# ScalarE empties the modulation's bank, branch B's last y loaded beside products, final projection's additions ahead of its scaling

## Chip, cores and metric

One NeuronCore of one Trainium2 chip runs the whole program. The metric is the device time of one launch in microseconds (us), median of several runs. TensorE (PE) does the matrix products, VectorE (DVE) and ScalarE (ACT) work element by element and read the products' PSUM banks, GpSimd (POOL) works on SBUF, and SyncE (SP) issues every DMA of this kernel, in one queue. Each engine runs its instructions strictly in the order of its own list.

## What is computed

Two layers of a bidirectional backbone over 1024 latent tokens and 256 context tokens of width 1024, batch 1, and a last RMSNorm. Layer 0 (even) has two branches, A (a gated linear recurrence, RG-LRU) and B (windowed attention). Layer 1 (odd) is HGRN2 in chunks. Cut to what matters:

```python
silu_c, silu_cc = silu(c), silu(c_ctx)
for layer in range(2):
    sh, sc, gt = split(silu_c @ ada_w[layer] + ada_b[layer], 3)     # the modulation
    mod_c = silu_cc @ ada_w[layer] + ada_b[layer]                   # and for the context
    u_lat = rmsnorm(h_lat, norm_w) * (1 + sc) + sh
    u_ctx = rmsnorm(h_ctx, norm_w) * (1 + sc_ctx) + sh_ctx
    # even: p = u @ w_in ; ya = rglru(conv(xa)) * silu(ga) ; yb = window_attention(q, k, v) * silu(gb)
    #       m = concat(ya, yb) @ w_out
    # odd:  o = gla_scan(forward) + gla_scan(backward) ; m = (rmsnorm(o) * silu(og)) @ w_out
    h_lat = h_lat + gt * m_lat
return rmsnorm(h_lat, final_norm_w)
```

Every product is in float32 split in two: a weight and an input are each a high and a low part, and a product is three passes (high by high, high by low, low by high).

## The kernel before

Activations lie transposed: 128 of the 1024 features on the partitions, tokens along a row. Tokens come in chunks c = 0, 1 (512 latent tokens each) and c = 2 (256 context tokens). An output block m is 128 features. A product of one block with one chunk is 8 input blocks k by three passes, 24 matmuls (`mm3`, line 104; `steps3` is the same with pauses).

**Weights.** `load_w` (lines 90 to 95) issues a DMA into `w_raw`, ScalarE casts it to `w_hi` and POOL subtracts for `w_lo`. Cast and subtraction are at high priority (`PRI_W` = 300).

**Order.** A planner orders each engine's list from program order and from planned times; `tc.high_priority(offset=n)` moves an instruction n places forward. Once made, each list is fixed. Inside `tc.manual_schedule(engines={PE.engine})` PE keeps program order; that holds for the attention, for layer 1 and for the end, but not for the RG-LRU loop nor for `out_B`.

**Modulation.** `ada_mm` (lines 155 to 168) makes a row of the modulation in a PSUM bank of the tag `ada`, of which there is one. ScalarE copies it out (line 167); `ada_fin` (line 173) transposes it on PE into the same bank (`ps_c`, line 175), and VectorE adds the bias from there into `mods` (line 177). The next `ada_mm` needs the bank again. In the RG-LRU loop over j = 0 to 7, each turn projects the next turn's X, then calls `ada_fin` for the row of the turn before, then makes gates with tanh, exp, square and root on ScalarE and scans on VectorE, and ends with a new `ada_mm`.

**Branch B's output.** After the attention, `load_yB(c)` (line 787) reads branch B's y for a chunk back from DRAM in 8 pieces: `split_y` (lines 690 to 694) issues a DMA into `yr` (3 buffers), casts on ScalarE (`y_hi`) and subtracts on VectorE or POOL in turn (`y_lo`). All three chunks are loaded, and then `out_B((2, 0), ...)` (line 772) issues the loads of `acc` (branch A's result, line 775) and goes through m = 0 to 7: weights, a product for chunk 2, one for chunk 0, an addition into `acc` out of the bank (line 781), and the sum of squares. The products have two banks (`mmo`). Chunk 1 comes in a second `out_B((1,), ...)`.

**The end.** The final projection's `out_m` (line 1045) makes a product, and VectorE adds it to the residual `h2` (line 1051); `sumsq` (lines 187 to 194) squares on ScalarE and adds up on VectorE (`n_ss`). In `out_early`, chunk 0 is done for head blocks k = 0 to 6 while the last head (h = 7) is still at work. Then a loop over m adds k = 7 to chunk 0 (three matmuls) and does the first half of chunk 1 (24 matmuls of 256 columns). `final_norm` (line 1107) is a generator in two steps: column sums `n_ps` on PE and the root, and then the spread `n_pr`, its copy `n_rs` (one buffer) and eight scalings of `h2` (line 1111) with the output's DMAs. Last come the eight products of chunk 1's second half, with the second steps of two norms between them, and its own norm. The products have four banks (`mm`).

```python
    for m in range(8):                                                   # lines 1124 to 1128
        w = ws[m] = load_m(m) if m > 1 else last_w[1 + m]
        SY.dma_start(h2[1][:, m], h1_d[:, m, 512:1024])
        drain(out_m(0, full, m, [(m, 7)], wk, ss[0]))
        drain(out_m(1, half[0], m, [(k, k) for k in range(8)], w, ss[1]))
```

Of the kernel before, what the change touches and what calls it, by code (L numbers as in the profile page):

```python
# [11 lines left out]
F32 = mybir.dt.float32  # L12
# [38 lines left out]
def backbone_kernel(ctx: ExitStack, tc: tile.TileContext, a: dict, out):  # L51
# [32 lines left out]
    def load_w(src, n=1024, tag="w", wp=wp0, split=False, bufs=(2, 3)):  # L84

        pad = [128, 1024 if tag == "w" else n]
        raw = wp.tile([128, n], F32, tag=tag + "_raw", name="w_raw", bufs=bufs[0], padded_shape=pad)
        hi, lo = (wp.tile([128, n], F32R, tag=f"{tag}_{p}", name=f"w_{p}", bufs=bufs[1], padded_shape=pad)
                  for p in ("hi", "lo"))
        SY.dma_start(raw, src)  # L90

        for o, m, eng in ((0, n // 2, V), (n // 2, n, G)) if split else ((0, n, G),):
            with tc.high_priority(offset=PRI_W):
                S.copy(hi[:, o:m], raw[:, o:m])  # L94
                eng.tensor_tensor(out=lo[:, o:m], in0=raw[:, o:m], in1=hi[:, o:m].bitcast(F32), op=ALU.subtract)  # L95
        return hi, lo
# [37 lines left out]
    def drain(*gens):  # L134
        for g in gens:
            for _ in g:
                pass
# [32 lines left out]
    def ada_mod(wpool, psp, l, g, bufs=NADA):  # L170
        ada_fin(psp, ada_mm(wpool, psp, l, g, bufs), l, g)

    def ada_fin(psp, row, l, g):
        pc = psp.tile([128, 512], F32, tag="ada", name="ps_c", bufs=1)
        PE.transpose(pc[:, :128], row, ident)
        with tc.high_priority(offset=PRI_E):
            V.tensor_tensor(out=mods[:, l, g], in0=pc[:, :128].rearrange("p (b x) -> p b x", x=32)[:, :, 0:2],
                            in1=adab[:, l, g].unsqueeze(2).to_broadcast([128, 4, 2]), op=ALU.add)
            if g < 4:
                V.scalar_tensor_tensor(out=amul[:, l, 2 * g:2 * g + 2], in0=mods[:, l, g, 2:4], scalar=1.0,  # L180
                                       in1=normw[:, l * 8 + 2 * g:l * 8 + 2 * g + 2].unsqueeze(2)
                                       .to_broadcast([128, 2, 2]), op0=ALU.add, op1=ALU.mult)
# [220 lines left out]
    for j in range(8):  # L403
# [20 lines left out]
        if j < 7:  # L424
            X_next = x_proj(j + 1)
        if j:
            ada_fin(psA, row, *ada_lg)
        R, I, A, M = ([rg.tile([128, W], F32, tag=t_, name=t_, bufs=2) for _ in range(2)] for t_ in "RIAM")

        for d in range(2):  # L430
# [338 lines left out]
    hp0, hp0_st = open_pool("hp0")  # L769
    acc, n1ss = {}, {}  # L770

    def out_B(cs, yB, npool, psp, tag, bufs):
        for c in cs:
            acc[c] = npool.tile([128, 8, CHUNKS[c][1]], F32, tag=f"acc{c}", name=f"acc{c}")
            SY.dma_start(acc[c], hA_d[c])
            n1ss[c] = npool.tile([128, CHUNKS[c][1]], F32, tag=f"n1ss{c}", name="n1ss")
        for m in range(8):
            w = load_w(a["wo0"][8 + m], split=cs == (1,))
            for c in cs:
                ps, gt = out_half(w, m, yB[c], c, psp, tag, bufs)  # L780
                V.scalar_tensor_tensor(out=acc[c][:, m], in0=ps, scalar=gt, in1=acc[c][:, m],  # L781
                                       op0=ALU.mult, op1=ALU.add)
                if c < 2:
                    SY.dma_start(h1_d[:, m, c * 512:c * 512 + 512], acc[c][:, m])
                sumsq(npool, n1ss[c], acc[c][:, m], m)

    def load_yB(c):
        yB[c] = new_y(c)
        for k in range(8):
            split_y(yrp, yb_d[k // 2][c][:, k % 2], CHUNKS[c][1], *yB[c], k)  # L790

    yB = {}
    load_yB(2)
    load_yB(0)
    load_yB(1)
    out_B((2, 0), yB, hp0, psB, "mmo", 2)
    psB_st.close()
    psC, psC_st = open_pool("psC", space=PSUM)
    hp, hp_st = open_pool("hp", side="right")
# [245 lines left out]
    def out_m(c, sl, m, ks, w, ss=None):  # L1045

        n = sl.stop - sl.start
        ps = psC.tile([128, 512], F32, tag="mm", name="mm_o", bufs=4)
        yield from steps3(ps[:, :n], [(w[0][:, i * 128:i * 128 + 128], w[1][:, i * 128:i * 128 + 128],
                                       yT[c][:, k, 0, sl], yT[c][:, k, 1, sl]) for i, k in ks], n)  # L1050
        V.scalar_tensor_tensor(out=h2[c][:, m, sl], in0=ps[:, :n], scalar=mods[:, 1, 4 + m // 4, m % 4, 0:1],  # L1051
                               in1=h2[c][:, m, sl], op0=ALU.mult, op1=ALU.add)
        if ss is not None:
            sumsq(fq, ss, h2[c][:, m, sl], m if sl.start == 0 else (m - 4) % 8)

    full = slice(0, 512)

# [66 lines left out]
    for m in range(8):  # L1124
        w = ws[m] = load_m(m) if m > 1 else last_w[1 + m]
        SY.dma_start(h2[1][:, m], h1_d[:, m, 512:1024])
        drain(out_m(0, full, m, [(m, 7)], wk, ss[0]))
        drain(out_m(1, half[0], m, [(k, k) for k in range(8)], w, ss[1]))
    norms = [final_norm(0, full, ss[0]), final_norm(1, half[0], ss[1])]
    for g in norms:  # L1130
        next(g)
    for m in (4, 5, 6, 7, 0, 1, 2, 3):
        if m in (6, 7):
            drain(norms.pop(0))

        drain(out_m(1, half[1], m, [(k, k) for k in range(8)], ws[m] if m > 3 else load_m(m), ss[2]))
# [90 lines left out]
```

## Time and profile before

| | |
|---|---|
| median of 3 runs | 1970.53 us (1968.96 to 1972.46) |
| the profiled execution | 1970.83 us, of which the span of its instructions is 1969.0 us |
| PE | 1877.2 us busy, 95% of the span |
| PEld (weight loads, beside PE) | 1599.7 us, 81% |
| VectorE, ScalarE, POOL | 1134.1 us (58%), 954.6 us (48%), 467.0 us (24%) |
| mean granted TensorE clock | 0.986 of full speed |

The page gives each engine's busy time; the view of waits says who waited for whom and how long; the view of windows gives busy time and granted clock in chosen stretches; the timeline lists instructions in order of time, with the idle time of their engine just before them and what ended it in brackets.

### The profile page before, as it was taken

Reading aid. Unit: us, or ns where it says so; the run is one execution under the profiler, and the core shown is the slowest. Engines: PE = TensorE matmul, PEld = TensorE weight load, DVE = VectorE, ACT = ScalarE, POOL = GpSimd, SP = SyncE. Lnnn points to the kernel's source line nnn. Section 1 sums busy time; section 2 is a strip of 40 time slices with the busy share of each in tenths; the row PEclk is TensorE's granted clock in tenths of the full one; section 3 lists DMA queues with packets and bytes.
Section 4 is the critical chain, followed back from the end, with each engine's and each line's share of the span. In section 5 each row is a group of like instructions: output and inputs, shape, how many; then the busy total and the mean of one; then the engine's idle time right before and its main releaser. Section 6 shows DMA issues by size and latency. Waiting matters only on the chain. (4 is left out here: it accounts for less than half of the span.)

```text
span 1969.0 us, 36589 instructions
## 1 busy us (share of the span) xinstructions
PE 1877.2 (95%) x15228; PEld 1599.7 (81%) x15228; DVE 1134.1 (58%) x1920; ACT 954.6 (48%) x1766; POOL 467.0 (24%) x309
## 2 busy tenths in 40 slices
PE   6989999999999999999998999999999999999896
PEld 5778888889888787788777889888887987888686
DVE  3766555554456555656534757375557447555656
ACT  4478666683146668555642442443443334334332
POOL 0133323330111114213232212121221122122342
PEclk8999999999999999999999999999999999999998
DMA  8222333322633436435435231111111101011643
GB/s 320 88 97 92 110 102 107 99 100 101 198 113 103 128 101 192 144 119 174 142 115 201 92 109 45 33 55 35 45 52 34 53 29 61 23 54 39 252 142 115
DMA packets 89462, 207.53 MB, mean 105 GB/s; under 512 B 9808, under 2 KB 38224, under 8 KB 88272
## 3 DMA queue, kind: packets, MB, share of 16 engines
q1 hardware_dynamic: 89296, 205.20, 31.6%
q8 instruction: 119, 1.95, 0.4%
q14 instruction: 47, 0.39, 0.1%
HBM read 155.36 MB, written 49.81 MB: 104 GB/s over the span
## 5 line engine op out<-in xcount | busy, mean ns | idle before, releaser
L95 POOL TENSOR_TENSOR w_lo<-w_raw,w_hi 128x1024 fp32r<-128x1024 f32 (+2 forms) x137 | 314.9, 2302 | 1109.3 <-ACT w_hi L94 1059.7
L104 PE MATMUL mm<-u_hi,w_hi 128*128 128x512 f32 (+1 forms) x1456 | 547.3, 376 | 6.7 <-DVE sga L423 3.7
L104 PE MATMUL mm<-u_lo,w_hi 128*128 128x512 f32 (+1 forms) x1456 | 527.6, 362 | 4.9 <-DVE u_lo L251 4.9
L104 PE MATMUL mm<-u_hi,w_lo 128*128 128x512 f32 (+1 forms) x1456 | 527.3, 362 | 0.0
L104 PEld LDWEIGHTS mm<-u_hi,w_hi 128*128 128x128 f32 x1456 | 276.1, 190 | 54.5 <-issue 9.3
L104 PEld LDWEIGHTS mm<-u_lo,w_hi 128*128 128x128 f32 x1456 | 276.8, 190 | 42.4 <-DVE u_lo L251 6.9
L104 PEld LDWEIGHTS mm<-u_hi,w_lo 128*128 128x128 f32 x1456 | 275.9, 189 | 43.2
L94 ACT CAST w_hi<-w_raw 128x1024 fp32r<-128x1024 f32 (+2 forms) x163 | 141.7, 884 | 195.3 <-PE mm L104 77.8
L104 PE MATMUL mmo<-y_hi,w_hi 128*128 128x512 f32 (+1 forms) x384 | 146.1, 380 | 7.4 <-DVE acc L781 7.4
L600 DVE CUSTOM_DVE_ANT_0 p<-s_ps,maskA 128x640 f32<-128x640 f32 (+2 forms) x160 | 110.4, 713 | 59.6 <-PE s_ps L595 59.5
L611 ACT ACTIVATE p<-p,nm 128x640 f32<-128x640 f32 (+2 forms) x160 | 118.7, 743 | 42.8 <-DVE nm L607 39.2
L104 PE MATMUL mmo<-y_hi,w_lo 128*128 128x512 f32 (+1 forms) x384 | 137.5, 358 | 0.0
L104 PE MATMUL mmo<-y_lo,w_hi 128*128 128x512 f32 (+1 forms) x384 | 137.0, 357 | 0.0
L628 ACT COPY pt<-t 128x512 f32<-128x512 f32 x168 | 94.7, 581 | 82.5 <-PE t L625 82.1
L104 PE MATMUL mm_v<-w_hi,u_hi 128*128 128x256 f32 x400 | 115.2, 288 | 0.0
L104 PE MATMUL mm_v<-w_lo,u_hi 128*128 128x256 f32 x400 | 113.1, 283 | 0.0
L104 PE MATMUL mm_v<-w_hi,u_lo 128*128 128x256 f32 x400 | 113.1, 283 | 0.0
L946 DVE TENSOR_TENSOR KK<-KK,tot 128x1280 f32<-128x1280 f32 x48 | 80.1, 1670 | 41.0 <-PE lv L932 23.9
L625 PE MATMUL t<-ident,p 128*128 128x128 f32 x672 | 98.5, 274 | 4.3 <-ACT pt L628 2.7
L104 PE MATMUL mm_o<-yT,w_hi 128*128 128x256 f32 (+1 forms) x384 | 92.1, 334 | 8.2 <-DMA yT<-y_d 3.1
L625 PEld LDWEIGHTS t<-ident,p 128*128 128x128 f32 x672 | 80.7, 141 | 19.1 <-ACT pt L628 4.7
L104 PEld LDWEIGHTS mmo<-y_hi,w_hi 128*128 128x128 f32 x384 | 73.4, 191 | 22.4 <-issue 8.1
(219 smaller groups left out, 3462.6 us busy)
## 6 DMA issues: line engine op xcount, KB each, us to landing
w_raw<-w_in SPq DMA_DIRECT2D x66, 512.0 KB, 3.7
ada<-ada_w_in SPq DMA_DIRECT2D x48, 512.0 KB, 6.4
w_raw<-wo_in SPq DMA_DIRECT2D x32, 512.0 KB, 3.7
qt<-q_d SPq DMA_DIRECT2D x20, 512.0 KB, 4.9
y_d<-yhl SPq DMA_DIRECT2D x14, 512.0 KB, 3.1
yT<-y_d SPq DMA_DIRECT2D x14, 512.0 KB, 11.0
w_raw<-wo1m_in SPq DMA_DIRECT2D x12, 512.0 KB, 3.8
xin<-hT_in SPq DMA_DIRECT2D x5, 1024.0 KB, 9.2
```

The costliest lines, as they stand in the source:

```text
L94: S.copy(hi[:, o:m], raw[:, o:m])
L95: eng.tensor_tensor(out=lo[:, o:m], in0=raw[:, o:m], in1=hi[:, o:m].bitcast(F32), op=ALU.subtract)
L104: ins = PE.matmul(ps, l, r, start=(first and i == 0), stop=(last and i == n - 1))
L600: V.tensor_tensor_reduce(out=p[:, :nk], in0=s_ps[:, c0[x]:c0[x] + nk], in1=self.msks[x], scale=1.0, scalar=NEG, op0=ALU.add, op1=ALU.max, ...
L611: S.activation(p, p, AF.Exp, scale=0.125, bias=nm[:, x:x + 1], accum_out=dn[:, x:x + 1])
L625: PE.transpose(pt[:, h], self.P[h][:, o:o + 128], ident)
L628: S.copy(ptc, pt)
L946: V.tensor_tensor(out=kv_, in0=kv_, in1=custom(tot, 1, [[2, nb // 2], [nb - 1, 2], [0, hb]]), op=ALU.mult)
```

## The change

Four edits. `ada_fin` gets a pool: within the RG-LRU loop, ScalarE copies the eight numbers that count (128x8) out of the bank, and VectorE adds from the copy. `load_yB` becomes a generator; chunks 2 and 0 are loaded at once as before, and chunk 1's eight pieces one by one, each behind the weights' load of one block m of `out_B((2, 0))`. In `out_m`, the addition and the sum of squares go to high priority (100 places). At the end, the two products of each m change places, and the first steps of the two norms come behind the first product of the second half rather than ahead of it.

```diff
-    def ada_fin(psp, row, l, g):
+    def ada_fin(psp, row, l, g, pool=None):
         pc = psp.tile([128, 512], F32, tag="ada", name="ps_c", bufs=1)
         PE.transpose(pc[:, :128], row, ident)
         with tc.high_priority(offset=PRI_E):
-            V.tensor_tensor(out=mods[:, l, g], in0=pc[:, :128].rearrange("p (b x) -> p b x", x=32)[:, :, 0:2],
+            mc = pc[:, :128].rearrange("p (b x) -> p b x", x=32)[:, :, 0:2]
+            if pool:
+                m_sb = pool.tile([128, 4, 2], F32, tag="m_sb", name="m_sb", bufs=2)
+                S.copy(m_sb, mc)
+                mc = m_sb
+            V.tensor_tensor(out=mods[:, l, g], in0=mc,
                             in1=adab[:, l, g].unsqueeze(2).to_broadcast([128, 4, 2]), op=ALU.add)
...
         if j:
-            ada_fin(psA, row, *ada_lg)
+            ada_fin(psA, row, *ada_lg, rg)
...
-    def out_B(cs, yB, npool, psp, tag, bufs):
+    def out_B(cs, yB, npool, psp, tag, bufs, beside=None):
...
         for m in range(8):
             w = load_w(a["wo0"][8 + m], split=cs == (1,))
+            if beside:
+                next(beside)
...
             split_y(yrp, yb_d[k // 2][c][:, k % 2], CHUNKS[c][1], *yB[c], k)
+            yield
 
     yB = {}
-    load_yB(2)
-    load_yB(0)
-    load_yB(1)
-    out_B((2, 0), yB, hp0, psB, "mmo", 2)
+    drain(load_yB(2), load_yB(0))
+    out_B((2, 0), yB, hp0, psB, "mmo", 2, load_yB(1))
...
-        V.scalar_tensor_tensor(out=h2[c][:, m, sl], in0=ps[:, :n], scalar=mods[:, 1, 4 + m // 4, m % 4, 0:1],
-                               in1=h2[c][:, m, sl], op0=ALU.mult, op1=ALU.add)
-        if ss is not None:
-            sumsq(fq, ss, h2[c][:, m, sl], m if sl.start == 0 else (m - 4) % 8)
+        with tc.high_priority(offset=PRI_E):
+            V.scalar_tensor_tensor(out=h2[c][:, m, sl], in0=ps[:, :n], scalar=mods[:, 1, 4 + m // 4, m % 4, 0:1],
+                                   in1=h2[c][:, m, sl], op0=ALU.mult, op1=ALU.add)
+            if ss is not None:
+                sumsq(fq, ss, h2[c][:, m, sl], m if sl.start == 0 else (m - 4) % 8)
...
+        drain(out_m(1, half[0], m, [(k, k) for k in range(8)], w, ss[1]))
         drain(out_m(0, full, m, [(m, 7)], wk, ss[0]))
-        drain(out_m(1, half[0], m, [(k, k) for k in range(8)], w, ss[1]))
     norms = [final_norm(0, full, ss[0]), final_norm(1, half[0], ss[1])]
-    for g in norms:
-        next(g)
-    for m in (4, 5, 6, 7, 0, 1, 2, 3):
-        if m in (6, 7):
+    for i, m in enumerate((4, 5, 6, 7, 0, 1, 2, 3)):
+        if i == 1:
+            for g in norms:
+                next(g)
+        if i in (2, 3):
             drain(norms.pop(0))
```

## Rows read from the trace of the kernel before

**Rows 1.** The page, part 1: busy us, share of the span, instructions
```profile
PE 1877.2 (95%) x15228; PEld 1599.7 (81%) x15228; DVE 1134.1 (58%) x1920; ACT 954.6 (48%) x1766; POOL 467.0 (24%) x309
```

**Rows 2.** PE's waits, whole span: us in total, times, longest
```profile
PE mmo L104 <- DVE acc L781: 7.4, 2, 6.8
...
PE ps_m L164 <- DVE mods L177: 5.0, 1, 5.0
```

**Rows 3.** Windows: length, then busy us (x instructions) of PE to POOL, clock, DMA
```profile
141.70:147.00 5.30, 5.29 (x14) 3.64 (x14) 0.00 (x0) 2.89 (x4) 0.08 (x1) 0.50 0.73 247
...
1039.20:1042.00 2.80, 2.75 (x13) 2.75 (x14) 1.27 (x1) 1.46 (x3) 2.23 (x2) 0.50 0.97 302
...
1893.20:1898.90 5.70, 5.70 (x25) 5.51 (x26) 1.28 (x2) 0.63 (x1) 0.00 (x0) 0.50 0.00 0
...
1930.10:1933.00 2.90, 2.90 (x15) 2.90 (x15) 0.17 (x1) 0.26 (x1) 0.00 (x0) 0.50 0.02 6
```

**Rows 4.** Timeline, second turn of the RG-LRU loop: start, us, engine, instruction [idle before]
```profile
141.50 0.15 DVE L177 TENSOR_TENSOR mods<-ps_c,c_adabT 128x8 f32<-128x8 f32 x1
...
141.71 0.63 PE L164 MATMUL ps_m<-ada,cc 128*32 128x128 f32 x2 [5.04 <-DVE mods L177]
...
143.96 0.69 ACT L437 ACTIVATE I<-gate,rgb 128x512 f32<-128x512 f32 x1 [6.22 <-PE gate L104]
```

**Rows 5.** Timeline, ScalarE: a copy out of the modulation's bank
```profile
106.49 0.27 ACT L167 COPY adar<-ps_m 128x128 f32<-128x128 f32 x1
```

**Rows 6.** Timeline, SP and VectorE at the start of branch B's output
```profile
1027.50 0.33 SPq L90 DMA_DIRECT2D w_raw<-wo_in  x1
1029.20 1.57 SPq L692 DMA_DIRECT2D yr<-yb_d  x3
1030.81 0.42 SPq L775 DMA_DIRECT2D acc<-hA_d  x1
...
1038.71 0.48 DVE L781 SCALAR_TENSOR_TENSOR acc<-mmo,mods,acc 128x256 f32<-128x256 f32 x1 [1.23 <-DMA acc<-hA_d]
```

**Rows 7.** Groups by line: operation x count, busy us, mean ns, idle before
```profile
L694 POOL TENSOR_TENSOR y_lo<-yr,y_hi 128x512 fp32r<-128x512 f32 (+1 forms) x24 | 27.8, 1160 | 25.2 <-ACT y_hi L693 24.7 <-PE pv L639 0.3
```

**Rows 8.** Timeline, end of the last head and start of the final loop
```profile
1890.23 2.36 POOL L95 TENSOR_TENSOR w_lo<-w_raw,w_hi 128x1024 fp32r<-128x1024 f32 x1 [5.56 <-ACT w_hi L94]
1890.70 3.03 DVE L1036 TENSOR_TENSOR yT<-on,yT 128x512 fp32r<-128x512 f32 x2
...
1890.72 0.49 PE L104 MATMUL mm_o<-yT,w_hi 128*128 128x512 f32 x1 [1.03 <-ACT yT L1035]
1893.18 0.79 PE L104 MATMUL mm_o<-yT,w_hi 128*128 128x512 f32 x1 [1.97 <-DVE yT L1036]
```

**Rows 9.** Timeline, block m = 2 of the final loop and its weights
```profile
1901.35 1.03 ACT L94 CAST w_hi<-w_raw 128x1024 fp32r<-128x1024 f32 x1
...
1902.45 2.38 POOL L95 TENSOR_TENSOR w_lo<-w_raw,w_hi 128x1024 fp32r<-128x1024 f32 x1 [9.87 <-ACT w_hi L94]
...
1904.89 0.38 PE L104 MATMUL mm_o<-yT,w_lo 128*128 128x256 f32 x1 [1.10 <-POOL w_lo L95]
1905.11 0.40 PE L104 MATMUL mm_o<-yT,w_hi 128*128 128x256 f32 x2
1905.35 0.28 PE L104 MATMUL mm_o<-yT,w_lo 128*128 128x256 f32 x1
```

**Rows 10.** Timeline, PE: column sums of the two norms
```profile
1927.11 1.02 PE L212 MATMUL n_ps<-ones_m,n_ss 128*128 128x1 f32 x8 [1.13 <-DVE n_ss L194]
1929.34 0.76 PE L212 MATMUL n_ps<-ones_m,n_ss 128*128 128x1 f32 x4 [1.21 <-DVE n_ss L194]
```

**Rows 11.** Timeline, the last projection's end
```profile
1940.94 9.73 DVE L1111 SCALAR_TENSOR_TENSOR h<-h,fnw,n_rs 128x512 f32<-128x512 f32 x8
...
1951.21 0.48 PE L104 MATMUL mm_o<-yT,w_hi 128*128 128x256 f32 x2 [1.96 <-ACT n_rs L231]
...
1960.06 0.77 PE L212 MATMUL n_ps<-ones_m,n_ss 128*128 128x1 f32 x4 [2.93 <-DVE n_ss L194]
```

## The prediction

> **What bounds the kernel now.** I read the page first: PE is busy for 95% of the span and no other engine passes 58% [rows 1]. PE's records overlap, so 95% alone proves little; but in the 25 us windows PE is busy all through most stretches, so what a change can win is PE's idle time and what follows it, and it has to be looked for stretch by stretch. The second view is PE's waits. The two longest single ones are a wait of the modulation's product for VectorE, 5.0 us, and one of branch B's output, 6.8 us [rows 2]. Third, windows around the idle places: behind four of them the granted clock is 0.50, the lower of the two levels (1.2 for 2.4 GHz), though PE is busy all through [rows 3]. Such a stretch costs about half of its length on top of the idle time. Fourth, the timeline there, for which engine is late and what stands in its queue. The four edits fall on five such places, A to E.
>
> **A, the copy in the RG-LRU loop.** In the second turn PE stops for 5.04 us because the single modulation bank is still to be read by VectorE's addition, and this stands in VectorE's queue behind the scans, until 141.50 [rows 4]. The 5.3 us after it run at half clock [rows 3]: half of that is 2.65; part of the stretch isn't paced by matmul columns, so I count 2.2. At stake: 5.0 + 2.2 = 7.2 us (7.7 at most). ScalarE has finished its list and is idle from 143.96 - 6.22 = 137.74 [rows 4]; a copy from this bank takes 0.27 us [rows 5]. At the latest, then, the bank is free at 138.0, against 141.65 now, and PE wants it at 141.71 - 5.04 = 136.67: at most 1.35 us of idle time is left, at best none. I take 0.5, with the clock kept, since that is nearer to a copy standing ahead of the sigmoids. Gain 6.7. Cost: seven turns have such a copy, 7 x 0.27 = 1.9 us of ScalarE's time. ScalarE is at 48% [rows 1], but behind the copy the sigmoids wait that empty the gates' banks, and PE waits for those; between 0 and 1.9 I take 0.4, because in most turns PE has other products to go on with. VectorE's addition now waits for ScalarE too; behind it VectorE has only work that waits for the gates anyway. A: **6.3 us**, ends 1.8 (3.7 and no clock, less 1.9) and 7.7.
>
> **B, chunk 1's y beside the products.** PE waits 6.8 us for the addition into acc, and 0.6 in a second wait [rows 2]; half of the slow 2.8 us is 1.4 more [rows 3]. At stake: 8.8 us. The addition comes late because acc's DMA does: issued at 1030.81, it has landed by 1038.71, 7.9 us later [rows 6]. In SP's queue it stands behind three pieces of chunk 1 (1029.20), which wait for yr buffers, that is for casts and subtractions of pieces before. The edit takes those out of its way. acc then goes at the latest right behind the weights of 1027.50, near 1027.9, or earlier where its memory is free earlier, which the trace doesn't show. With the same 7.9 us it lands at 1035.8, 2.9 us earlier; with no yr pieces on the DMA engines beside it, it should need less, and if it goes before 1021 nothing is left of the wait. Ends: 1.6 (only the step from 1029.20 to 1030.81) and 8.8. I take 6.0: issue near 1027.9, some 5 us to land (an estimate from the 7.9 with its company gone), half a us of PE idle left for each of two waits, and the clock kept. The moved steps: eight yr DMAs now stand in SP's queue each behind one block's weights, with eight casts on ScalarE and eight subtractions, POOL's the dearer at 1.16 us [rows 7]; the work that hides them is a block's 24 matmuls of 256 columns and 24 of 512, by the 0.12 us of the first [rows 9] about 2.9 + 5.8 = 8.7 us. A cast that waits for its piece has the next squares behind it, and for those only the norm waits. If that cover failed for the last piece, chunk 1 would start late by no more than acc's 7.9 us.
>
> **C, the two products of a block change places.** At the loop's start PE needs the last head's y, chunk 0, and waits 1.03 and 1.97 us for its high and low part [rows 8]; the 5.7 us behind run at half clock and cost 2.85 [rows 3]. At stake: 5.85. In the new order PE begins with chunk 1's product at 1890.72 - 1.03 = 1889.69: heads 0 to 6 are 21 matmuls at 0.12 us (two start 0.24 apart [rows 9]), 2.5 us of work that needs nothing of the last head. It then wants chunk 1's low part, the second of VectorE's two subtractions, which ends at 1893.73 [rows 8]. So 1.5 us of idle time remains in place of 3.0. Whether the clock still falls for it, the trace of before can't say; I take it as kept. 1.5 + 2.85 = **4.3 us**; ends 1.5 (the clock falls all the same) and 5.85. Against it: block m = 2 already waits 1.10 us for its weights' low part [rows 9], and the three chunk-0 matmuls that used to stand ahead (0.7 us) now come behind. Between 0 and 0.7 I take off 0.5.
>
> **D, the norms' first steps one product later.** The column sums find VectorE's sums not ready: 1.13 and 1.21 us idle [rows 10], then 2.9 us at half clock, 1.45 [rows 3]. At stake: 3.8. Now a product of 24 x 0.12 = 2.9 us comes between. The later sum was ready at 1929.34, which is 3.4 us after the last product's end (1927.11 - 1.13 = 1925.98), so 0.5 to 0.8 stays. **3.0 us**, ends 1.5 and 3.8.
>
> **E, additions ahead of scalings.** Eight scalings hold VectorE from 1940.94 for 9.73 us; the additions that free PE's banks come behind, and PE stops for 1.96 us [rows 11] (the view names ScalarE's n_rs, which waits for the same scalings). At the very end PE waits 2.93 us for the last sum [rows 11], of which some 1.2 is backlog (an estimate: an addition of 256 columns takes 0.48 us [rows 6], square and sum of the same size at most as much, with hops 1.7). At stake: 3.2. VectorE's work doesn't get less; only its order changes, and the planner may still put late scalings ahead of the last addition. Ends 0 and 3.2; **1.7 us**. In `out_early` the additions move ahead of a head's VectorE steps: under 1 us each (512 columns, twice the 0.48), either sign, counted at nothing since products cover it.
>
> There is a rule to weigh at E. The row first: of the two subtractions at 1890.70 the pair took 3.03 us while POOL's w_lo ran from 1890.23 to 1892.59 [rows 8]; the eight scalings took 1.22 us each, also beside weights [rows 11]. The Trainium skill (SBUF — State Buffer, "Who interferes with whom") says that a VectorE instruction with two SBUF inputs is blocked for as long as a GpSimd instruction reading SBUF holds the shared port; the trace agrees. By it scalings and sums are held by the four last w_lo in any order, and only the additions, with one input in PSUM, gain by moving. By the first reading E is 1.7 us, by the rule alone 0.
>
> **Sum.** 6.3 + 6.0 + 4.3 - 0.5 + 3.0 + 1.7 = 20.8 us. PE is the bound between these places, so each gain moves all that follows. The sum stands against the profiled execution, 1970.83 us, 0.3 above the median of 1970.53; from the median, 1949.7 us.
>
> **Rivals.** (1) *Waits shrink but stay.* acc lands only 2.9 us earlier, and the clock still falls at C: 3.1 + 2.8 us less, 1955.6. For it: other transfers crowd the DMA engines at B; against: the pieces that crowded them most are gone. (2) *The backlog on VectorE stays*: the mechanism of the rows at E, scalings beside w_lo at 1.22 us each; E gives 0, 1951.4. (3) *A new stall from the new plan.* The RG-LRU loop and out_B are ordered by the planner, and A's own stall is the kind that it leaves behind: 7.2 us apiece. One such, 1956.9; two, 1964. For it: one more ScalarE instruction per turn and eight moved loads; against: PE has no other wait above 3 us now. (4) *Slower: weights behind squares.* With the squares at high priority and chunk 1's product first, the cast of block m + 1 could stand behind the last square of block m in ScalarE's list. From a block's end that is an addition and a square of 512 columns, some 0.7 us each (an estimate from the 0.48 for 256 [rows 6]), cast 1.03 and w_lo 2.38 [rows 9], 4.8 us, with only two matmuls as cover. For six blocks it is 28 us, and the time 1978; it decides from 3.5 us a block on (20.8 / 6). For it: m = 2 does so once already, at 1.10 us; against: casts have priority 300 against 100 and stand earlier in the program. (5) *The edits change nothing that counts*: the copy stands as late in ScalarE's list as the addition did in VectorE's, acc stays behind: within 3 us of before.
>
> **Chances.** Forecast with (2): 0.64. (1): 0.15. (3): 0.11. (4): 0.06. (5): 0.04. The range of 8 in 10 goes from 1942 (all upper ends but 1 us) to 1964 (lower ends, two new stalls). Four us (0.2%) are about what a measurement of this kernel can tell from no change: faster 0.91, same 0.03, slower 0.06.
>
> **What would show it.** A: no PE wait for the modulation above 1.4 us, and clock 1.00 from 137 to 147. B: acc's DMA ahead of chunk 1's pieces, PE's wait for acc under 3 us. C: PE starts the final loop with 256 columns and waits once, about 1.5 us. D: both column sums idle for under 1 us together. E: no PE idle time between the last products, tail of PE's wait under 2.9 us. Wrong it would be if a wait of several us stood where none was, in the loop's later turns or before w_lo in the final loop.

## The result, and the profile after

The changed kernel takes **1960.04 us** (median of 7 runs, 1952.12 to 1962.55) against 1970.65 us for the kernel before (7 runs, 1968.54 to 1972.46): ratio 0.994, 95% interval 0.9927 to 0.9952, that is 10.6 us less. The sum had promised 20.8 us. The sign and the range held; half of the gain is missing. The profiled execution of after took 1962.55 us, the longest of the seven (span 1960.8, against 1969.0 before), so the two traces are 8.3 us apart, and it is these 8.3 us that the comparison by stretches below has to explain.

Part 1 of the page of after answers [rows 1]; PE is at 96% instead of 95%:

```profile
PE 1878.5 (96%) x15228; PEld 1602.8 (82%) x15228; DVE 1140.4 (58%) x1920; ACT 954.4 (49%) x1773; POOL 468.7 (24%) x309
```

PE's waits in after (us in total, times, longest), which answer [rows 2]:

```profile
PE n_ps L217 <- DVE n_ss L199: 5.6, 1, 5.6
...
PE mmo L104 <- DVE acc L788: 2.8, 2, 2.2
...
PE mm_o L104 <- POOL w_lo L95: 2.5, 2, 1.9
...
PE gate L104 <- ACT I L442: 1.6, 1, 1.6
PE mm_o L104 <- ACT w_hi L94: 1.3, 1, 1.3
```

The modulation's 5.0 us are gone and acc's 7.4 us are 2.8. Four waits are new or longer: 5.6 us for the last sum (2.93 before), 1.3 and 1.9 us for a block's weights in the final loop (1.10 before), and 1.6 us for a gate.

Where the time went is read by setting the start of PE's n-th instruction in one trace against the n-th of the other; PE's list has the same length in both, and only a few products change places in it. The shift of after against before, in us (negative is earlier), at the end of each stretch:

| stretch | shift at its end | share of it | forecast |
|---|---|---|---|
| second RG-LRU turn to branch B (A) | -5.8 | -5.8 | -6.3 |
| start of branch B's output (B) | -10.8 | -5.0 | -6.0 |
| layer 1 to the final loop, untouched by the change | -4.6 | **+6.2** | 0 |
| start of the final loop, to y's arrival (C) | -9.9 | -5.3 | -4.3 |
| blocks 0 to 3 of it (C's price) | -4.6 | **+5.3** | +0.5 |
| column sums (D) | -8.7 | -4.1 | -3.0 |
| last half, to PE's last product (E) | -11.1 | -2.4 | -1.7 with the next line |
| last sum, scaling and output (E's price) | -8.3 | **+2.8** | |

Windows of after (length, busy us of PE, PEld, DVE, ACT, POOL, granted clock, DMA share, GB/s), which answer [rows 3]: the RG-LRU turn, branch B, the final loop's start, its block 2, the column sums:

```profile
136.50:142.50 6.00, 5.01 (x52) 3.61 (x51) 6.00 (x6) 4.25 (x9) 2.93 (x1) 1.00 0.06 25
1029.60:1033.00 3.40, 3.40 (x18) 3.40 (x17) 0.00 (x0) 0.00 (x0) 0.32 (x1) 0.50 0.96 397
1882.00:1890.00 8.00, 6.49 (x45) 5.74 (x45) 5.76 (x8) 2.19 (x3) 2.40 (x1) 1.00 0.21 82
1896.60:1903.40 6.80, 6.11 (x25) 5.85 (x26) 1.66 (x2) 1.03 (x2) 5.75 (x3) 0.50 0.73 215
1920.00:1932.00 12.00, 12.00 (x102) 11.87 (x102) 5.89 (x10) 5.03 (x10) 4.79 (x2) 1.00 0.15 44
```

The fall of the clock is gone at A, at y's arrival and at the column sums. It stayed at B, and it came back at 1896.6, at the waits for block 2's weights, for 6.8 us, of which PE was busy for 6.1 (5.7 us of busy time had been slowed at the loop's start before).

**The second turn of the RG-LRU loop** (answers [rows 4, 5]):

```profile
136.96 0.16 ACT L180 COPY m_sb<-ps_c 128x8 f32<-128x8 f32 x1
...
141.10 1.37 ACT L443 ACTIVATE M<-R,sneg 128x1284 f32<-128x1284 f32 x1 [1.61 <-DVE M L466]
...
142.40 0.15 DVE L182 TENSOR_TENSOR mods<-m_sb,c_adabT 128x8 f32<-128x8 f32 x1
...
143.09 0.50 PE L104 MATMUL gate<-uh,w_hi 128*128 128x512 f32 x1 [1.58 <-ACT I L442]
```

The copy stands ahead of the sigmoids, takes 0.16 us and frees the bank at 137.12; VectorE's addition is as late as ever, and PE no longer cares. PE then waits 1.58 us for a gate's bank: in ScalarE's list an activation of M stands ahead of the sigmoids that empty the gates, and it waits 1.61 us for VectorE.

**Branch B** (answers [rows 6]): SP's queue and PE.

```profile
1021.65 0.33 SPq L90 DMA_DIRECT2D w_raw<-wo_in  x1
1022.03 1.94 SPq L780 DMA_DIRECT2D acc<-hA_d  x2
1024.03 0.91 SPq L697 DMA_DIRECT2D yr<-yb_d  x2
...
1028.82 0.38 PE L104 MATMUL mmo<-y_hi,w_hi 128*128 128x256 f32 x1 [2.24 <-DVE acc L788]
```

acc goes right behind the weights and ahead of chunk 1's pieces, 8.8 us earlier than in [rows 6]; 5.8 us of that are A's shift, so that B's own part is 3.0 us. It needs 6.2 us to land:

```profile
acc<-hA_d SPq DMA_DIRECT2D x1, 1024.0 KB, 6.2
```

**The final loop's start and block 2** (answers [rows 8, 9]; PE, ScalarE and POOL in order of time):

```profile
1888.83 0.38 PE L104 MATMUL mm_o<-yT,w_hi 128*128 128x256 f32 x1 [1.51 <-DVE yT L1042]
...
1893.77 1.03 ACT L94 CAST w_hi<-w_raw 128x1024 fp32r<-128x1024 f32 x1
1894.71 0.63 ACT L198 ACTIVATE n_sq<-h 128x512 f32<-128x512 f32 x1
...
1894.85 0.50 PE L104 MATMUL mm_o<-yT,w_hi 128*128 128x256 f32 x2 [1.27 <-ACT w_hi L94]
1894.88 7.47 POOL L95 TENSOR_TENSOR w_lo<-w_raw,w_hi 128x1024 fp32r<-128x1024 f32 x3 [7.25 <-ACT w_hi L94]
...
1897.29 0.58 PE L104 MATMUL mm_o<-yT,w_lo 128*128 128x256 f32 x1 [1.93 <-POOL w_lo L95]
```

PE waits once for y, 1.51 us, as worked out. Then block 2's cast starts only at 1893.77, because three squares of the blocks before it stand ahead of it in ScalarE's list; POOL's w_lo follows the cast, and PE waits for both. In before the cast stood behind three squares too:

```profile
1900.81 0.64 ACT L193 ACTIVATE n_sq<-h 128x512 f32<-128x512 f32 x1 [0.54 <-DVE h L1051]
```

What changed is the work that PE had left meanwhile. The last of the three was then chunk 0's square of block 1, and behind that product PE still had chunk 1's 24 matmuls of block 1 and three of block 2, some 3.6 us. Now it is chunk 1's square, and behind that product only chunk 0's three matmuls are left, 0.7 us. From that product's end to the end of w_lo it is 4.8 us in before and some 4.4 us in after.

**The end** (answers [rows 11]):

```profile
1938.18 2.40 POOL L95 TENSOR_TENSOR w_lo<-w_raw,w_hi 128x1024 fp32r<-128x1024 f32 x1 [3.13 <-ACT w_hi L94]
1938.23 2.90 DVE L1118 SCALAR_TENSOR_TENSOR h<-h,fnw,n_rs 128x512 f32<-128x512 f32 x1
...
1941.06 0.74 DVE L1118 SCALAR_TENSOR_TENSOR h<-h,fnw,n_rs 128x512 f32<-128x512 f32 x1
...
1947.25 0.47 DVE L1058 SCALAR_TENSOR_TENSOR h<-mm_o,mods,h 128x256 f32<-128x256 f32 x1
...
1948.61 0.48 DVE L1058 SCALAR_TENSOR_TENSOR h<-mm_o,mods,h 128x256 f32<-128x256 f32 x1
...
1949.97 0.48 DVE L1058 SCALAR_TENSOR_TENSOR h<-mm_o,mods,h 128x256 f32<-128x256 f32 x1
...
1951.56 0.98 PE L217 MATMUL n_ps<-ones_m,n_ss 128*128 128x1 f32 x4 [5.58 <-DVE n_ss L199]
```

PE is through with its products at 1945.99, without the stop of 1.96 us. But VectorE still owes three additions, and they follow each other 1.36 us apart, since each has the sum of the block before it ahead in the list, which waits for that block's square. The gain reappears as a longer wait for the last sum. The first two scalings shown tell where VectorE's time went: the one that starts beside POOL's w_lo takes 2.90 us and ends 0.5 us after it, the next takes 0.74 us.

### The profile page after: what moved, and what is told of

It reads as the page before. It is cut to its first block, busy times and chain, and to the rows that moved or that the text cites. A ratio compares the mean times of both kernels' runs of the same rounds, so it can differ in the third digit from the quotient of the medians.

```text
span 1960.8 us, 36587 instructions
## 1 busy us (share of the span) xinstructions
PE 1878.5 (96%) x15228; PEld 1602.8 (82%) x15228; DVE 1140.4 (58%) x1920; ACT 954.4 (49%) x1773; POOL 468.7 (24%) x309
## 4 chain that ended last, share of the span: by engine, by line
PE 77%; DVE 12%; ACT 4%; DMA 3%; issue 2%; POOL 1%; SPq 1%; ACTq 0%; DVEq 0%; POOLq 0%
PE mm L104 36%; PE mmo L104 9%; PE mm_v L104 7%; PE pv L644 4%; PE t L630 3%; PE mm_o L104 3%; PE gate L104 3%; PE s_ps L599 2%; PE pv L983 2%; PE s_ps L600 2%; PE lv L926 1%; PE po L1013 1%; DVE uc L415 1%; PE po L1015 1%; PE po L1014 1%
## 5 line engine op out<-in xcount | busy, mean ns | idle before, releaser
L622 POOL COPY rd<-dn 128x128 f32<-128x128 f32 x80 | 24.7, 308 | 271.9 <-DVE dn L619 114.8
```

## The experiments

A measure that is free of what happens earlier is used beside the run times: the **end stage**, from the end of the last head's last transposes on PE to the end of the span. It is 79.3 us before and 76.1 us in after. All ratios are to the kernel before, timed on the same chip in the same series: its median was 1971.57 us for the first four kernels (23 runs), 1969.44 us for the next four (8 runs) and 1971.03 us for the last three (7 runs). The three series ran on three chips, so kernels of different series are compared by their ratios; the changed kernel's is 0.994.

**The changed kernel once more**, unaltered.

> The changed kernel once more, unaltered. Theory 1 (chance): in its first trace the granted clock fell to 0.50 behind four PE gaps that the change does not touch (near 1142, 1446, 1620 and 1797 us) and that are as long in the kernel before, where it fell behind one of them; this is chance of the single execution, so in this trace the set of gaps with a fall is another one, PE's gaps are the same within 0.3 us, and the times spread over some 10 us in step with the mean granted clock (0.985 to 0.990). Theory 2 (caused): the change itself makes the clock fall there, so the same four places fall again and the time is 1960 to 1963.

1960.31 us (1954.98 to 1961.99), ratio 0.9946 [0.9928, 0.9963]; the traced execution has a span of 1957.0 us, 3.8 under that of after. In layer 1 waits and work agree; the granted clock doesn't. Windows of after, then of this execution, behind two waits that are 2.61 and 2.41 us long in both:

```profile
1618.00:1629.00 11.00, 8.39 (x37) 7.70 (x37) 7.98 (x15) 2.79 (x11) 3.59 (x1) 0.69 0.03 12
1792.00:1801.00 9.00, 6.59 (x30) 5.66 (x29) 9.00 (x10) 3.13 (x5) 5.69 (x2) 0.81 0.17 51
```

```profile
1618.00:1629.00 11.00, 8.39 (x54) 7.46 (x54) 9.31 (x21) 3.49 (x11) 3.59 (x1) 1.00 0.03 10
1792.00:1801.00 9.00, 6.58 (x42) 5.59 (x41) 8.43 (x15) 3.15 (x11) 3.99 (x2) 1.00 0.16 53
```

In 11 us PE gets 54 matmuls done at 1.00 and 37 at 0.69, behind the same idle time. So what after lost in layer 1 is chance of the one execution. All 13 traces (before, after, and one for each kernel of this section) have four such waits there (1.78, 2.60, 2.60 and 2.41 us, equal to 0.04 us everywhere). The clock fell behind the first in 10 of them, the second in 5, the third in 6, the fourth in 2. Half-rate time in layer 1 was 3.4 us in the trace of before, 17.1 us in that of after, and 3.4 or 6.8 us in the eleven others; (17.1 - 3.4) / 2 = 6.8 us is near the 6.2 us lost.

**Part A alone.**

```diff
+            if pool:
+                m_sb = pool.tile([128, 4, 2], F32, tag="m_sb", name="m_sb", bufs=2)
+                S.copy(m_sb, mc)
+                mc = m_sb
...
-            ada_fin(psA, row, *ada_lg)
+            ada_fin(psA, row, *ada_lg, rg)
```

> Of the change only ScalarE's copy out of the modulation's bank. Predicted part A: 6.3 us less than before, 1964.3; PE's gap of 5.03 us near 137 gone, a new one of about 1.6 us behind the gates, and the clock full from 137 to 148. Rival: the seven copies delay the gates in later turns, and the gain is under 3 us.

1965.08 us (1963.56 to 1966.55), ratio 0.9969 [0.9958, 0.9979]: 6.5 us by the medians. The one wait left in that turn is 1.56 us, for the gate. A stands by itself, at its forecast size.

**Part B alone.**

```diff
-    load_yB(2)
-    load_yB(0)
-    load_yB(1)
-    out_B((2, 0), yB, hp0, psB, "mmo", 2)
+    drain(load_yB(2), load_yB(0))
+    out_B((2, 0), yB, hp0, psB, "mmo", 2, load_yB(1))
```

> Of the change only the loading of chunk 1's y beside products. Predicted part B: 6 us less than before, about 1964.6; from the first trace of the changed kernel I expect PE's wait for acc to be 2.2 us rather than 6.8 and the part to be worth 5. Rival: the eight pieces beside the products cost back what acc's earlier load gains, and the time is within 2 us of before.

1967.66 us (1962.18 to 1972.95), ratio 0.999 [0.9979, 1.0001]. By run times alone B can't be told from nothing; in the trace it is worth 3.7 us, and the wait that stays is this one (6.8 us in [rows 2]):

```profile
1035.23 0.58 PE L104 MATMUL mmo<-y_hi,w_hi 128*128 128x256 f32 x1 [3.07 <-DVE acc L783]
```

**Parts C, D and E alone.**

> Of the change only the edits at the end: products of a block exchanged, first steps of the norms one product later, additions and squares at high priority. Predicted parts C, D and E: 4.3 - 0.5 + 3.0 + 1.7 = 8.5 us less than before, 1962. From the first trace of the changed kernel I expect only 3 to 5 us: C gives nothing, since block m = 2 waits 3.2 us for its weights and the clock falls there, D gives 4, E nothing, since VectorE's backlog makes the last wait 5.6 us rather than 2.9. Rival: the losses at m = 2 and at the end come from the other edits' shifts, and alone the end gives its 8.5 us.

1967.98 us (1966.48 to 1973.32), ratio 0.9983 [0.9972, 0.9994]: 3.6 us by the medians, where 8.5 us were forecast for the three. The end stage is 76.2 us, as in after, with the same waits (1.51, 1.26, 1.93 us and 5.87 us at the end). So the losses of the end come from the end's own three edits, not from A or B.

**All eight blocks' weights kept** through the second half of the final projection, on top of the change.

```diff
-        return load_w(a["wo1m"][m], tag="fw", wp=fq, bufs=(3, 4))
+        return load_w(a["wo1m"][m], tag="fw", wp=fq, bufs=(3, 6))
...
-        drain(out_m(1, half[1], m, [(k, k) for k in range(8)], ws[m] if m > 3 else load_m(m), ss[2]))
+        drain(out_m(1, half[1], m, [(k, k) for k in range(8)], ws[m], ss[2]))
```

> The changed kernel, but all eight blocks' weights stay in memory through the final projection's second half (four weight loads, casts and w_lo subtractions fewer there); everything else is as in the changed kernel, whose end stage (from the end of the last head's transposes to the end of the span) takes 76.1 us and whose last sum is waited for 5.6 us. Theory: the additions came late because VectorE's scalings and sums ran beside POOL's w_lo and each took up to twice its time; without the w_lo the scalings take some 0.7 us each, the last additions follow the products, PE waits 2 to 3 us for the last sum, the end stage is about 73 us and the time 2.6 to 3.6 us under the changed kernel's (about 1957). Rival: the wait comes from the order in VectorE's list, where each addition has the sum of the block before it ahead, 1.36 us apart; then it stays above 4.5 us and the time is that of the changed kernel.

1953.64 us (1952.58 to 1955.29), ratio 0.9917 [0.9901, 0.9933]; end stage 70.1 us. VectorE and PE at the end:

```profile
1930.60 2.07 DVE L1118 SCALAR_TENSOR_TENSOR h<-h,fnw,n_rs 128x512 f32<-128x512 f32 x3
...
1943.58 0.48 DVE L1058 SCALAR_TENSOR_TENSOR h<-mm_o,mods,h 128x256 f32<-128x256 f32 x1 [1.38 <-PE mm_o L104]
...
1945.08 0.61 PE L217 MATMUL n_ps<-ones_m,n_ss 128*128 128x1 f32 x4 [1.54 <-DVE n_ss L199]
```

The scalings of 512 columns take 0.69 us each; in after some took 2.90. The last addition now waits for PE, not PE for it, and the last wait is 1.54 us. The backlog was VectorE's, and POOL's four w_lo made it. (Four casts on ScalarE are gone as well, but in after ScalarE sat idle for VectorE ahead of the squares of the last blocks.) The rival (the order of additions and sums) falls: each addition still has the sum of the block before it ahead. The gain of 6 us in the end stage is larger than expected: 4.0 us come from the wait, some 1.4 us from a shorter fall of the clock at block 2 (3.4 us of PE's busy time against 6.1).

**Casts of blocks 2 and 3 ahead of the squares**, on top of the change.

```diff
-    ws = {}
+    ws = {m: load_m(m) for m in (2, 3)}
...
+        if m == 0:
+            with tc.issue_after(load_w.cast):
+                drain(*parts)
```

> The changed kernel, but the weights of blocks 2 and 3 are called for ahead of the final loop and block 0's squares are placed behind their casts in ScalarE's list. Theory: the exchange of a block's two products won its 1.5 us and lost it to block 2's weights, whose cast stood behind the squares of block 0. Then PE's waits of 1.27 and 1.93 us for w_hi and w_lo of block 2 are gone, the one of 1.5 us for the last head's y stays, and the end stage takes 72.9 us if the clock still falls behind that one wait, down to about 70 if it doesn't; time 3.2 to 6.6 us under the changed kernel's. Rival: the wait only moves, to the weights of block 3 or 4, or to the squares, and the end stage stays at 76.

1957.64 us (1952.10 to 1961.44), ratio 0.9935 [0.9911, 0.9958]; end stage 75.4 us. Both waits for block 2's weights are gone, and a new one stands in their place:

```profile
1879.95 7.92 POOL L95 TENSOR_TENSOR w_lo<-w_raw,w_hi 128x1024 fp32r<-128x1024 f32 x3 [5.55 <-ACT w_hi L94]
...
1880.42 5.22 DVE L1042 TENSOR_TENSOR yT<-on,yT 128x512 fp32r<-128x512 f32 x2
...
1885.70 0.58 PE L104 MATMUL mm_o<-yT,w_hi 128*128 128x256 f32 x1 [3.66 <-DVE yT L1042]
```

The three w_lo now run back to back while VectorE makes the last head's y. Its pair of subtractions takes 5.22 us (2.48 and 2.82, each beside a w_lo), 3.03 in [rows 8] (2.43 beside the one w_lo, then 0.68); PE waits 3.66 us for y instead of 1.51. The end stage was expected at 70 to 72.9 us. The rival was right that the wait moves, though not where to: of the weights behind, PE waits for one w_lo alone, 0.74 us.

**acc in two pieces a chunk**, on top of the change.

```diff
-            SY.dma_start(acc[c], hA_d[c])
...
+        for c, o in [(c, o) for o in (slice(0, 2), slice(2, 8)) for c in cs]:
+            SY.dma_start(acc[c][:, o], hA_d[c][:, o])
```

> The changed kernel, but branch B's acc is loaded in two pieces for each chunk, blocks 0 and 1 first, then the other six. Theory: what is left of B's wait (2.24 and 0.58 us for acc, and 3.4 us at half clock behind it) is the 6.1 us that a whole 1 MB chunk takes to land, and its issue waits for the last block of branch A's output; the first pieces of 0.25 and 0.5 MB land before PE needs them, the wait is under 0.5 us and the clock is kept: 2.5 to 4.5 us under the changed kernel's time. Rival: the landing is set by the traffic on the DMA engines (0.93 to 1.09 busy share there) whatever the size of a piece; then the wait stays at 2 us or above.

1960.70 us (1956.47 to 1961.98), ratio 0.9955 [0.9940, 0.9970]: no gain. PE still waits 3.36 us. PE, SP's queue, and the issues from 1021 us on with KB each and median us to landing:

```profile
1028.07 0.39 PE L104 MATMUL mmo<-y_hi,w_hi 128*128 128x256 f32 x1 [3.36 <-DVE acc L789]
...
1021.90 0.38 SPq L90 DMA_DIRECT2D w_raw<-wo_in  x1
1022.33 2.01 SPq L782 DMA_DIRECT2D acc<-hA_d  x4
```

```profile
acc<-hA_d SPq DMA_DIRECT2D x1, 1536.0 KB, 10.5
...
acc<-hA_d SPq DMA_DIRECT2D x1, 768.0 KB, 7.3
...
acc<-hA_d SPq DMA_DIRECT2D x1, 512.0 KB, 5.9
acc<-hA_d SPq DMA_DIRECT2D x1, 256.0 KB, 5.1
```

The forecast of the theory fails, and the wait is what the rival gave. But size isn't without effect. The four pieces were issued some 0.5 us apart and land one behind the other, the last of 1.5 MB some 3.7 us after the one before it: about 2.5 us for each MB, as for the chunks in after (2 MB land 4.9 us behind 1 MB). The first piece needs 1 us less than the whole chunk in after, no more, because the weights' 0.5 MB stand ahead of either; and PE was at this place 1.9 us earlier than in after (1024.7 against 1026.6), so that it waits longer. What keeps SP from issuing acc before 1022 (memory that comes free, or the weights' DMA ahead of it) was not settled.

**The three edits before in one.**

> The edits of the three kernels before it in one: weights kept, casts of blocks 2 and 3 ahead of the squares, acc in two pieces. Theory: each loss has a place of its own, so the gains add up: 8 to 14 us under the changed kernel's time, about 1949, end stage 67 to 69.5 us. Rival: they share a cause (the clock, or VectorE's backlog that takes up what is won ahead of it), and the sum is less than the largest two.

1955.26 us (1953.75 to 1957.61), ratio 0.9926 [0.9909, 0.9943]; end stage 69.7 us, 0.4 us under that with the weights kept alone, since the wait of 3.67 us for y is there again. The gains don't add up; only the kept weights carry.

**The change without E.**

```diff
-        with tc.high_priority(offset=PRI_E):
-            V.scalar_tensor_tensor(out=h2[c][:, m, sl], in0=ps[:, :n], scalar=mods[:, 1, 4 + m // 4, m % 4, 0:1],
...
+        V.scalar_tensor_tensor(out=h2[c][:, m, sl], in0=ps[:, :n], scalar=mods[:, 1, 4 + m // 4, m % 4, 0:1],
```

> The changed kernel without part E: the final projection's additions and sums have no priority over the scalings, all else as in the changed kernel (end stage 76.1 us, last sum waited for 5.6 us). Theory (VectorE's backlog sets the end in any order): PE's stop of about 2 us for the additions is back, its wait for the last sum shrinks to about 3, the end stage stays within 1 us of 76.1 and the time within 2 us of the changed kernel's; block 2's waits for its weights, 1.27 and 1.93 us, stay, since the squares stand before the cast without the priority too. Rival (E does gain, and something else lengthened the end): end stage 78 or more. Second rival (E's priority put the squares before block 2's cast): those waits go, end stage about 73.

1955.15 us (1953.99 to 1957.36), ratio 0.9922 [0.9907, 0.9937]; end stage 74.0 us. PE's two waits in the last half:

```profile
1936.01 0.48 PE L104 MATMUL mm_o<-yT,w_hi 128*128 128x256 f32 x2 [1.97 <-ACT n_rs L236]
...
1945.07 0.58 PE L217 MATMUL n_ps<-ones_m,n_ss 128*128 128x1 f32 x4 [1.64 <-DVE n_ss L199]
```

Together 3.6 us, 2.0 us less than the 5.58 us with E. In this execution the stop cost 3.4 us at half clock besides (1.7 us), so that the balance is near nought: the end stage is 0.4 us shorter than in the execution with acc in pieces, whose end is the changed kernel's and whose clock fell as long at block 2 (3.4 us; 74.4 us), and 2.1 us shorter than in after (6.8 us there). The waits of 1.27 and 1.93 us for block 2 are there without E too. By the run times the kernel is 3.5 us faster than the changed one (0.9922 against 0.994), where under 2 us were expected; the intervals overlap, so it is shown that E gains nothing, and open whether it costs time.

**The change without C** (a block's products in the order of before).

```diff
+        drain(out_m(0, full, m, [(m, 7)], wk, ss[0]))
         drain(out_m(1, half[0], m, [(k, k) for k in range(8)], w, ss[1]))
-        drain(out_m(0, full, m, [(m, 7)], wk, ss[0]))
```

> The changed kernel with a block's two products in the order of before, chunk 0's first; all else as in the changed kernel. Theory (part C gave with one hand and took with the other): the waits of 1.0 and 2.0 us for the last head's y are back, block 2's waits for its weights shrink from 1.27 + 1.93 to about 1.1, the end stage is within 1 us of 76.1. Rival (the weights' waits come from the new priority, not from the exchange): those waits stay and the end stage is 77.5 to 79.

1957.53 us (1956.51 to 1960.10), ratio 0.9935 [0.9920, 0.9949]; end stage 73.3 us. PE's waits at the loop's start and at block 2:

```profile
1886.06 0.49 PE L104 MATMUL mm_o<-yT,w_hi 128*128 128x512 f32 x1 [1.03 <-ACT yT L1041]
...
1888.52 0.50 PE L104 MATMUL mm_o<-yT,w_hi 128*128 128x512 f32 x1 [1.97 <-DVE yT L1042]
...
1897.73 0.39 PE L104 MATMUL mm_o<-yT,w_lo 128*128 128x256 f32 x1 [1.11 <-POOL w_lo L95]
```

4.1 us of idle time against 4.7 us with C, by the very waits of [rows 8, 9]. C gives 1.5 us at y and takes 2.1 us at the weights. The end stage came out 2.8 us under the 76.1 us expected. That is no more than the clock explains: in this execution it didn't fall in the loop at all, in after it was halved for 6.1 us of PE's busy time, which is 3 us. Behind the waits of 1.03 and 1.97 us the clock fell in two of the four executions that have them (before and B alone; not A alone, nor here). Behind C's waits at block 2 it fell in all six executions that have them, for 3.4 or 6.8 us. So C gains nothing, in idle time or by the clock.

**Weights kept, casts early, and blocks 2 and 3's w_lo on VectorE** behind its last subtraction for y.

```diff
-        for o, m, eng in ((0, n // 2, V), (n // 2, n, G)) if split else ((0, n, G),):
+        for o, m, eng in ((0, n // 2, V), (n // 2, n, G)) if split else ((0, n, E),):
...
-    ws = {}
+    with tc.issue_after(load_w.sub):
+        ws = {m: load_m(m, V) for m in (2, 3)}
```

> The kernel with all eight blocks' weights kept, and besides the casts of blocks 2 and 3 ahead of block 0's squares, with those two blocks' w_lo on VectorE, placed behind its last subtraction for the last head's y, so that POOL reads no weights while VectorE makes that y. Theory (the casts' place cost 3.2 us, and in the kernel with early casts the w_lo on POOL only held up VectorE's subtractions): the wait for y is 1.5 us again, not 3.7; no wait for block 2's weights; the end stage 2 to 5 us shorter than with the weights kept alone, time about 1949 to 1952. Rival (a wait of about 3 us turns up wherever the weights are made): the two w_lo on VectorE hold the additions and PE waits for banks or for block 2 all the same; end stage as with the weights kept alone.

1952.66 us (1950.26 to 1954.89), ratio 0.9907 [0.9889, 0.9925]: the fastest of all, 18.4 us under before, though its interval overlaps that of the weights kept alone. End stage 68.8 us. VectorE and PE:

```profile
1892.11 2.35 DVE L95 TENSOR_TENSOR w_lo<-w_raw,w_hi 128x1024 fp32r<-128x1024 f32 x2
...
1886.64 0.39 PE L104 MATMUL mm_o<-yT,w_hi 128*128 128x256 f32 x1 [1.52 <-DVE yT L1042]
1893.38 0.38 PE L104 MATMUL mm_o<-yT,w_lo 128*128 128x256 f32 x1 [1.74 <-DVE w_lo L95]
```

The wait for y is back at 1.52 us: with one w_lo on POOL beside it the pair of subtractions takes 3.07 us again, not 5.22. Block 2 waits 1.74 us instead of 3.2, because VectorE's list still puts two additions of the loop ahead of the w_lo. The end stage is only 1.4 us shorter than with the weights kept alone, not 2 to 5, and the clock's fall there (3.4 us), which this execution doesn't have, is worth 1.7 us. So beyond the kept weights no gain is shown: the casts' place had cost half of the wait for block 2, but the engine that takes the work over has a queue of its own.

## Why the prediction was right, and where not

**What bounds the kernel** was read rightly: PE's gaps, and the clock behind them, are what the change moves, and each of the five places showed a change. Sign and range held, but the range was 22 us wide; the sum itself promised twice what came.

**A held**, 5.8 us in the trace and 6.5 us alone against 6.3. The bank came free at 137.12 (138.0 at the latest, by the text), and PE waits for it no more, where 0.5 us had been left. The copy took 0.16 us; 0.27 us came from a larger one. PE's wait for sigmoids, put at 0.4 us for the copies, is 1.58 us, but it isn't the copy's doing: VectorE's backlog, which had held the addition, now holds ScalarE, whose next activation waits 1.61 us for VectorE.

**B was mostly right.** acc goes where the text put it: 1022.03 in after is 1027.8 in the time of before (shift 5.8), against "near 1027.9". The step that failed is the landing, "some 5 us": it took 6.2 us in after, and PE's wait of "half a us" was 2.24 us; in the seven other executions with the same code there it took 6.3 to 8.1 us, and PE waited 2.4 to 4.2 us. Rival 1, other transfers on the DMA engines, came nearer: the weights' 0.5 MB stay ahead of acc in the queue, and in after its 1 MB lands some 2.5 us behind them. The clock fell as before, though it was taken as kept. What makes the landing differ by 2 us from execution to execution stays open. Nor does the entry of 6.0 us follow from its terms: 8.8 us at stake, less two waits of half a us, is 7.8 us. That the entry is near the 5.0 us measured is in part luck.

**C failed in the term "between 0 and 0.7 I take off 0.5"**, and with it in the value taken for the clock. The 1.5 us for y came out to a hundredth, and the clock stayed at 1.00 there. But block 2's weights cost 1.27 + 1.93 = 3.2 us where 1.10 us had been. What failed is the cover. The exchange was counted as three matmuls less ahead of block 2 (0.7 us); but the cast follows the square of whichever product comes first in block 1, and that is now the long one, so the 24 matmuls that had hidden cast and w_lo are behind PE when they start: 3.6 us of cover became 0.7 us. Rival 4 had this mechanism and its size for one block (4.8 us with hardly any cover), and set it aside by a comparison of priorities, though the cast stood behind a square in before already, as its own "for it" says. It struck once, not six times, so its price was 2.1 us of idle time, and here the fall of the clock, not 28 us. The kernel with the casts ahead of the squares has neither of the two waits. By the kernel without it, C adds 0.6 us of idle time where it was to save 3.8 us; and of those, 2.85 us were a fall of the clock that came in two of four executions.

**D did better than its term**, 4.1 us against 3.0, by the shift in the trace: no idle time stays at the column sums (0.5 to 0.8 us had been left), and the clock stays up. D was not run by itself.

**E is the rival that came true**: +0.4 us in the trace for a forecast of -1.7, the sum of -2.4 us at PE's stop and +2.8 us at the last sum. VectorE's time was the bound of the last half, as rival 2 had it, and neither of the two orders of its list changes that: without E PE waits 3.6 us, with it 5.58 us, and the end comes no earlier. The rule of the Trainium skill (SBUF — State Buffer, "Who interferes with whom") that spoke against E agrees with three measurements: a scaling of 512 columns that takes 2.90 us beside w_lo and 0.74 us right after it, subtractions of 2.48 and 2.82 us beside w_lo and 0.68 us without, and the whole backlog gone with four w_lo fewer. The means in the prediction (1.22 us for a scaling, 3.03 us for a pair) hide this: in before two of the eight scalings took 2.9 us each and six 0.74 us, so VectorE isn't slowed there but stopped until POOL's instruction is through. The forecast took E's 1.7 us and gave the rule's 0 a place inside the range; it should have been the other way round, since two rows already showed it.

**Outside the sum** stand the 6.2 us of layer 1. They belong to no step of the change: the waits there are those of before, and the same kernel a second time had two of the four falls. Nothing in the single trace of before could say that such falls are a matter of chance; it showed one behind four like waits, which was the hint. With the usual 6.8 us at half rate instead of 17.1 the profiled execution of after would be some 5 us shorter, about 1957.

Put together: of the 12.5 us that the traces lack against the sum (20.8 - 8.3), 6.2 are layer 1's chance, 3.8 C, 2.1 E, 1.0 B and 0.5 A, with D 1.1 us better. By the medians, in which layer 1's chance is averaged, the shortfall is 10.2 us; how much of that is clock and how much idle time can't be told apart from the run times alone.

## What to carry to other kernels

When an edit brings work forward on the engine that is the bound, look for what comes due next on *every* queue that feeds it (here the cast of the block after next), find what stands ahead of it in its list, whatever the priorities, and count how much work the bound engine has left from there on. Reordering an engine that is itself late at the end of a program moves its wait but doesn't shorten it; taking away what slows it, here weight splits on POOL beside VectorE, gave more in the end stage (6 us) than C, D and E together (3.2 us). A sum that takes "the clock kept" at several places should carry the fall as a loss at each of them, with a chance.

## What the hardware showed that was not expected

- Behind waits of PE that are equal to 0.04 us in 13 executions, the granted clock fell sometimes and sometimes not (10, 5, 6 and 2 times of 13 behind waits of 1.78, 2.60, 2.60 and 2.41 us). The shortest of the four had the most falls. Each fall of 3.4 us costs 1.7 us, and the changed kernel's runs spread over 10.4 us (1952.12 to 1962.55).
- In after and with acc in pieces, transfers that SP issued close together landed one behind the other, at about 2.5 us for each MB (1.5 MB 3.7 us behind the piece ahead of it, 2 MB 4.9 us behind 1 MB). So a first piece of 0.25 MB, with the weights' 0.5 MB ahead, took 5.1 us to land, where the whole 1 MB had taken 6.2 us.
- An instruction of VectorE with two inputs of 512 columns in SBUF that met POOL's w_lo ended some 0.5 us after it, early or late as it had started: a scaling took 2.90 us where the next took 0.74 us, a subtraction 2.48 us where another took 0.68 us. In a row of three w_lo beside two such subtractions POOL pays too: 2.40 us for the first, 2.8 us for the two others.
